# Where weight casts and inner operands stand in a Strassen-like MoE kernel's orders

## Chip, cores and metric

One Trainium2 chip, one NeuronCore of it. The metric is the device time of one execution in microseconds (us), from three runs of the kernel; beside them stands one profiled execution, with its own time and its trace. All times below are of the kernel before the change.

## What is computed

Soft routing over eight experts: every token goes through every expert, and the results are added with the softmax of the router's logits as weights. There are 8192 tokens of 512 features, and each expert is a 512x2048 matrix.

```python
probs = softmax(router_logits)                      # (16, 512, 8)
for e in range(8):
    expert_out = np.matmul(x, expert_weights[e])    # (16, 512, 512) @ (512, 2048)
    output += probs[:, :, e:e+1] * expert_out
```

Since the weight of an expert multiplies a whole row of x, this is one matrix product: a row of the left operand is (p_0 x, p_1 x, ..., p_7 x) with 4096 entries, and the right operand is the eight expert matrices on top of each other. The left operand is built on chip in float16, transposed; sums are accumulated in float32.

## The kernel before

**Products.** The big product is taken apart by a Strassen-Winograd scheme of seven products, numbered r = 1 to 7. Their right operands are blocks of the weights (11, 12, 21, 22: which half of the experts, which half of the columns) or sums of such blocks; their left operands are made from rows 256 at a time, for 16 pairs q of such row blocks. A product (r, q) is 256 rows by 1024 columns with a depth of 2048. It is done by the same scheme once more, in seven **steps** (1, 5, 6, 2, 7, 3, 4). A step is eight matmuls of 128x128 by 128x512 on TensorE. What a step leaves in PSUM is added up on VectorE or copied by ScalarE (`post`).

**Left operands.** A product's left operand `Left` has four tiles: t0 and t1 (x times a probability, one VectorE instruction each, tile `z` from `xT` and `pT`), s2 (tile `d`, a difference of the halves of t0, used by step 6), and the inner operand **i** = t1 minus s2 (tile `z` from `z,d`), used by steps 7 and 3.

**Stages and slots.** Stages are lists of one or two products; their steps alternate. In a stage of two products there are 14 slots: slot 2j is step j of the first product, slot 2j+1 is step j of the second. Stages 0 to 5 are pairs of product 1; stage 6 is product 2 of q = 13 and product 1 of q = 14; stage 7 is product 2 of q = 14 and product 1 of q = 15; stages 8 to 14 are pairs of product 2; stage 15 begins product 5. "Slot (7, 11)" below is slot 11 of stage 7. Hooks put by `at(stage, slot, make)` run ahead of a slot's matmuls.

**Third level.** In stages 0 to 5 and 8 to 12 (`thirds`) steps 1 and 5 of both products are taken together by the scheme once more, on 256 columns (`Third`, `Split`). This takes the place of slots 0 to 3. Its left sums are the tile **s** (four parts), its right sums the tiles **t** (eight parts for the first such stage of a right operand, `splits[2].queue` at slot (7, 2)). In `run_third` the parts m are written "x5", "q7" and so on: x for step 1, q for step 5. The last two slots of the stage before (`held`) are run in between: x1 x5 q1 q5, held slot 12, x2 q2 x6 q6, held slot 13, x7 q7 x3 q3 x4 q4. After x6 and q6 VectorE adds two halves in PSUM (`ps` from `ps,d`), and x7 and q7 write the half that was read there.

**VectorE's order** is written out by hand. All of its instructions stay in program order. Work that isn't the evacuation of a slot is a `Task` with an estimated cost in a deque, `queue`; `later` appends one. After each slot's matmuls `slack` takes tasks from the front for as long as VectorE's estimated clock is 0.3 us behind TensorE's (1.73 us a slot); then the slot's own evacuation is issued. A step that wants a task's result calls `need`, which takes everything in front of it too. `run(stage)` begins with `queue_i` for the stage's products, which appends their i tasks; the left operands of the next stage (t0, then s, s2, t1) are queued behind slot 0 or the part of it in a third-level stage.

**Background sums** are tasks of weights. A `wedge` makes three right operands from blocks 12 and 22 (sums with block 11) for one quarter-block of the weights: two casts from the float32 weights in HBM into the two halves a and b of one `w` tile, then three sums, t3 = b - a (into a tile `u`), t1 = (block 11) - a, t2 = b + a, each sent to a DRAM tile `wd` for later. Six wedges stand at stages 4 to 9; their sums are queued at slot 11 of the same stage (the last one at slot (10, 6)). `odd_t` at slot (12, 5) queues three sums of twice the size for a seventh place.

**Queues and buffers.** GpSimd issues the casts, the stores of results (`out_dram`), the partial results of product 1 (`kept`) and the `wd` stores, in program order; an entry that waits for its data or its buffer holds up what stands behind it. SyncE fetches and transposes; ScalarE's queue carries fetches of kept weights. The tiles `w`, `s`, `t` and `o` share one pool of 15 buffers: which buffer a new tile gets is settled by the order of the allocations (`new_w`, the `s` in `Third.make`, `new_t`), and its first writer waits until the earlier tile there has been read for the last time, by a matmul or by a store's landing.

The helper lines that the profile names are L112 (any VectorE tensor_tensor), L126 (any GpSimd DMA), L132 (any matmul), L180 (a fetch of kept weights), L627 and L638 (copies by ScalarE), L712 and L716 (the third level's copies).

Of the kernel before, what the change touches and what calls it, by code (L numbers as in the profile page):

```python
# [31 lines left out]
def kernel(  # L32
# [78 lines left out]
    def tt(o, a, b, op):  # L111
        dve(nc.vector.tensor_tensor(out=o, in0=a, in1=b, op=op))  # L112
# [29 lines left out]
    def new_z():  # L142
        return zpool.tile([P, K8, HQ], f16, name="z", tag="z")
# [248 lines left out]
    queue = deque()  # L392
    clock = {"pe": 0.0, "dve": 0.0}

    class Task:
# [5 lines left out]
        def run(self):  # L401
            self.done = True
            clock["dve"] += self.cost
            self.make()
# [10 lines left out]
    def later(cost, make, first=False):  # L415
        t = Task(cost, make)
        (queue.appendleft if first else queue.append)(t)
        return t

    def slack(slot=SLOT):  # L420
        if clock["pe"] > 30.0:
            clock["dve"] = max(clock["dve"], clock["pe"])
        clock["pe"] += slot
        while queue and clock["dve"] < clock["pe"] - LAG:
            queue.popleft().run()
# [66 lines left out]
    class Left:  # L492
# [48 lines left out]
                tt(self.s2, self.t[0][:, :, ds(HP, HP)], self.t[0][:, :, ds(0, HP)], SUB)  # L541
            self.task["s2"] = later(0.61, make)

        def queue_i(self):
            if self.into is not None:
                self.queue_make(1)

            def make():
                self.i = new_z()
                two = "p k (h t) -> p h k t"  # L550
                tt(self.i.rearrange(two, h=2), self.t[1].rearrange(two, h=2),
                   self.s2.unsqueeze(1).to_broadcast([P, 2, K8, HP]), SUB)
            self.task["i"] = later(1.14, make)

        def op(self, p):
            need(self.task[{1: 0, 5: 0, 6: "s2", 2: 1, 4: 1, 3: "i", 7: "i"}[p]])
# [194 lines left out]
    def at(stage, slot, make):  # L751
        hooks.setdefault((stage, slot), []).append(make)
# [47 lines left out]
    def product(r, q, **how):  # L800
        left, loads = left_of(r, q)
        lefts[r, q] = left
        p = None
        if r == 1:
            def sink(tn, o):
                pool(kept_rows(q)(tn), o)
            p = Product(right[1], left, sink)
        elif r == 2:
            if q >= 13:
                base = products[1, q].o.__getitem__  # L810
            else:
                base = bases[2, q] = Base(kept_rows(q))
            p = Product(right[2], left, to_out(q, 0, 0), base)
        elif r == 5:
            bases[6, q] = m1 = Base(kept_rows(q))
            m1.task = {}

            p = Product(right[5], left, to_out(q, 1, 0))
        elif r == 6:
            m1 = bases[6, q]  # L820

            def base(tn):
                need(m1.task[tn])
                return m1.t[tn]
            p = Product(right[6], left, to_out(q, 0, 1), base)
            if q in KEEP:
                left.kept = dram.tile([P, 2, K8, HQ], f16, name=f"kept_left_{q}")
        elif r == 7:
            if q < 14:
                base = bases[7, q] = Base(lambda tn: out_rows(q, 0, 1, tn))  # L830
            else:
                base = products[6, q].o.__getitem__
            p = Product(right[7], left, to_out(q, 1, 1), base)
        elif r == 4:
            p = Product(right[4], left, to_out(q, 1, 0, accum_op=ADD), products[7, q].o.__getitem__)
        else:
            p = Product(right[3], left, to_out(q, 0, 1, accum_op=ADD), **how)
        p.loads = loads
        products[r, q] = p
        return p  # L840
# [54 lines left out]
    def before(stage, n):  # L895
        for make in hooks.get((stage, n), ()):
            make()

    def after(stage, n):
        if n == 1:  # L900
            queue_lefts(stage + 1)
        if n == late.get(stage, 1):
            start_loads(stage + 2)
        if n == 5:
            store_loads(stage + 1)
        if n == 7:
            finish_loads(stage + 2)

    def run_third(stage):
        t = thirds[stage]  # L910
        before(stage, 0)
        t.parts("x1", "x5", "q1", "q5")
        after(stage, 1)
        before(stage, 1)
        held.pop(0)()
        after(stage, 2)
        t.parts("x2", "q2", "x6", "q6")
        before(stage, 2)
        held.pop(0)()
        after(stage, 3)  # L920
        before(stage, 3)
        t.parts("x7", "q7", "x3", "q3", "x4", "q4")
        for p in THIRD:
            for product in (t.a, t.b):
                product.post(p)
        after(stage, 4)

    def run(stage):
        some = stages[stage]
        for p in some:  # L930
            p.left.queue_i()
        slots = [(p, i) for i in range(len(some[0].steps)) for p in some]

        def one(n):
            p, i = slots[n]
            before(stage, n)
            p.step(p.steps[i])
            slack()
            p.post(p.steps[i])
            after(stage, n + 1)  # L940
        first = 0
        if stage in thirds:
            run_third(stage)
            first = 4
        end = len(slots) - (2 if stage + 1 in thirds else 0)
        for n in range(first, end):
            one(n)
        for n in range(end, len(slots)):
            held.append(lambda n=n: one(n))
# [23 lines left out]
    some = product(6, 15)  # L973
# [5 lines left out]
    some = product(4, order7[-1])  # L979
# [28 lines left out]
    def wedge(kn, e):  # L1008

        t = new_w()  # L1010
        a, b = t[:, ds(0, C), :], t[:, ds(C, C), :]
        rows = ds(e * C, C)

        casts = [lambda: cast_w(12, kn, e, a), lambda: cast_w(22, kn, e, b)]

        def send(what, u):
            to_kept(what, kn, e, u)

        def t3():
            u = new_u().rearrange("p (c two) t -> p c (two t)", two=2)  # L1020
            tt(u, b, a, SUB)
            send("t3", u)

        def t1():
            tt(a, b11[kn][:, rows, :], a, SUB)
            send("t1", a)

        def t2():
            tt(b, b, a, ADD)
            send("t2", b)  # L1030
        return casts, [t3, t1, t2]

    def wedge_at(stage, slot, kn, e, then):
        made = []

        def begin():
            casts, made_ = wedge(kn, e)
            casts[0]()
            made.extend(made_ + casts[1:])

        def go_on():
            for make in made[:3]:
                later(1.14, make)
        at(stage, slot, begin)
        at(stage, slot + 4, lambda: made[3]())
        at(*then, go_on)

    b21, t1, t2, t3 = {}, {}, {}, {}
# [19 lines left out]
    sums_at(5, 8, 2, b21, (7,))  # L1068
    sums_at(5, 12, 2, b21, (4,))
    for i, (kn, e) in enumerate((kn, e) for kn in ((0, 0), (1, 0), (1, 1)) for e in range(2)):  # L1070
        wedge_at(4 + i, 3, kn, e, {5:(10,6)}.get(i,(4+i,11)))

    def fetch_at_w(stage, slot, of, what, kn):
        at(stage, slot, lambda: of.__setitem__(kn, fetch_w(what, kn)))
# [4 lines left out]
    made = {}  # L1079
# [236 lines left out]
    for k in range(len(stages)):  # L1316
        run(k)
# [28 lines left out]
```

## Time and profile before

| what | value |
|---|---|
| three runs | 1364.66, 1365.53, 1365.61 us; median 1365.53 |
| the profiled execution | 1364.02 us, with a span of 1362.1 us from its first to its last instruction |
| granted TensorE clock | 1.00 over the whole span |
| HBM | 214.47 MB read, 167.97 MB written, 281 GB/s over the span |
| DMA queues, share of 16 engines | software (GpSimd) 56.7%, SyncE 32.3%, ScalarE 8.0% |

In the lines of a timeline the first two numbers are start and length in us; then come engine, line, operation and the tiles (written <- read); "x" is how many instructions were merged, and the bracket says how long the engine had been idle and what ended it. "PEld" is the load of a matmul's stationary operand. The end of a matmul is modelled, so neighbours overlap by a little, and the time from start to start is what a matmul costs. A `q` behind an engine's name is a DMA issued by it. The end of stage 7 and the beginning of stage 8 lie between about 205 and 240 us of the span.

### The profile page before, as it was taken

What the parts mean: (1) busy time and instruction counts of PE and PEld (TensorE: products, weight loads), DVE (VectorE), ACT (ScalarE), POOL (GpSimd) and SP (SyncE); (2) the same over time, 40 slices, a digit from 0 to 9 for tenths busy, and PEclk for the clock granted to TensorE, in tenths of its full rate; (3) what the DMA queues carried; (4) which work ended last, traced back from release to release, by engine and by line L of the source; (5) the groups of instructions that cost most, each with busy time, mean ns of one, the idle gap of its engine ahead of it and who ended that gap; (6) DMA issues with size and microseconds to landing.
All of it is one profiled execution on the core that took longest, in us unless ns stands there. A gap on an engine that the chain in (4) does not pass through costs nothing.

```text
span 1362.1 us, 18545 instructions
## 1 busy us (share of the span) xinstructions
PE 1355.7 (100%) x6801; PEld 662.8 (49%) x6801; DVE 1149.8 (84%) x1415; ACT 203.6 (15%) x386; POOL 409.4 (30%) x644
## 2 busy tenths in 40 slices
PE   9999999999999999999999999999999999999998
PEld 4555545565444444444444444444444444456554
DVE  7976789988999788787887888888889797998873
ACT  3332311111011111111111100000000000123221
POOL 3123233322223333324332122332333322232232
PEclk9999999999999999999999999999999999999999
DMA  9999999999999999999999977988898979999897
GB/s 192 229 249 247 232 232 310 286 309 356 314 307 273 315 339 286 294 280 281 328 275 334 351 241 206 221 246 204 230 243 234 241 204 296 291 223 247 198 206 117
DMA packets 195691, 356.43 MB, mean 262 GB/s; under 512 B 53136, under 2 KB 87184, under 8 KB 191248
## 3 DMA queue, kind: packets, MB, share of 16 engines
q0 software_dynamic: 88048, 183.02, 56.7%
q1 hardware_dynamic: 99488, 132.25, 32.3%
q10 hardware_dynamic: 8064, 39.99, 8.0%
q8 instruction: 53, 0.87, 0.3%
q14 instruction: 38, 0.31, 0.1%
HBM read 214.47 MB, written 167.97 MB: 281 GB/s over the span
## 4 chain that ended last, share of the span: by engine, by line
PE 98%; DMA 1%; issue 1%; POOL 0%; DVE 0%; ACT 0%; POOLq 0%
PE ps L132 98%; DMA w<-in_expert_weights_dram 1%; DMA out_dram<-h 0%; POOL w L126 0%; POOL kept L126 0%; POOL out_dram L126 0%; DVE h L112 0%; ACT h L638 0%; ACT h L1270 0%; DVE ps L112 0%; POOL ident L216 0%; POOLq L126 0%; POOLq L216 0%; POOLq L1330 0%
## 5 line engine op out<-in xcount | busy, mean ns | idle before, releaser
L132 PE MATMUL ps<-w,z 128*128 128x512 f16 x5144 | 1098.4, 373 | 0.4 <-DMA w<-in_expert_weights_dram 0.3
L132 PEld LDWEIGHTS <-z 128*128 128x128 f16 x5280 | 516.4, 98 | 578.1 <-DMA w<-in_expert_weights_dram 0.5
L126 POOL DMA_DIRECT2D out_dram<-h x380 | 249.4, 662 | 739.5 <-ACT h L638 366.1
L112 DVE TENSOR_TENSOR h<-ps,h 128x512 f32<-128x512 f32 x415 | 284.3, 687 | 157.5 <-PE ps L132 137.2
L112 DVE TENSOR_TENSOR z<-xT,pT 128x2048 f16<-128x2048 f16 x216 | 261.7, 1218 | 2.9 <-DMA xT<-w 2.9
L132 PE MATMUL ps<-w,d 128*128 128x512 f16 x880 | 199.1, 379 | 0.0
L132 PEld LDWEIGHTS <-d 128*128 128x128 f16 x880 | 86.1, 98 | 100.3
L112 DVE TENSOR_TENSOR z<-z,d 128x2048 f16<-128x2048 f16 x110 | 131.6, 1217 | 0.0
L638 ACT COPY h<-ps 128x512 f32<-128x512 f32 x64 | 37.6, 587 | 492.5 <-PE ps L132 486.8
L112 DVE TENSOR_TENSOR w<-w 128x1024 f16<-128x1024 f16 (+2 forms) x88 | 100.1, 1146 | 0.8
L627 ACT COPY h<-ps 128x512 f32<-128x512 f32 x90 | 52.8, 587 | 282.8 <-PE ps L132 267.2
L112 DVE TENSOR_TENSOR d<-z 128x1024 f16<-128x1024 f16 x110 | 74.4, 687 | 1.4
L624 ACT COPY h<-ps 128x512 f32<-128x512 f32 x90 | 51.7, 590 | 126.7 <-PE ps L132 119.8
L126 POOL DMA_DIRECT2D kept<-h x56 | 30.6, 547 | 106.7 <-ACT h L627 72.7
L132 PEld LDWEIGHTS <-s 128*128 128x128 f16 x544 | 53.2, 98 | 10.8 <-issue 1.3
L126 POOL DMA_DIRECT2D wd<-w x78 | 46.5, 621 | 38.4 <-DVE w L112 32.6
L132 PE MATMUL ps<-t,s 128*128 128x256 f16 x408 | 55.7, 273 | 0.8 <-DVE ps L112 0.8
L126 POOL DMA_DIRECT2D w<-in_expert_weights_dram x65 | 48.8, 771 | 11.9 <-issue 8.0
L112 DVE TENSOR_TENSOR ps<-ps,d 128x256 f32<-128x256 f32 x68 | 28.4, 430 | 24.9 <-PE ps L132 24.8
L112 DVE TENSOR_TENSOR ps<-ps,h 128x512 f32<-128x512 f32 (+1 forms) x66 | 45.1, 687 | 4.4 <-PE ps L132 4.1
L112 DVE TENSOR_TENSOR u<-xT,pT 128x2048 f16<-128x2048 f16 x38 | 46.3, 1217 | 0.0
L112 DVE TENSOR_TENSOR h<-h 128x512 f32<-128x512 f32 (+2 forms) x69 | 45.2, 675 | 0.1
(63 smaller groups left out, 365.2 us busy)
## 6 DMA issues: line engine op xcount, KB each, us to landing
out_dram<-h POOLq DMA_DIRECT2D x380, 256.0 KB, 6.9
pT<-p_dram SPq DMA_DIRECT2D x125, 256.0 KB, 6.8
h<-kept SPq DMA_DIRECT2D x116, 256.0 KB, 7.9
w<-wd ACTq DMA_DIRECT2D x25, 1024.0 KB, 11.0
xT<-x SPq DMA_DIRECT2D x76, 256.0 KB, 6.5
w<-in_expert_weights_dram POOLq DMA_DIRECT2D x35, 512.0 KB, 10.4
wd<-w POOLq DMA_DIRECT2D x64, 256.0 KB, 6.3
h<-out_dram SPq DMA_DIRECT2D x60, 256.0 KB, 5.6
```

Source lines behind the costliest of these rows:

```text
L112: dve(nc.vector.tensor_tensor(out=o, in0=a, in1=b, op=op))
L126: note(nc.gpsimd.dma_start(out=o, in_=i, **how))
L132: note(nc.tensor.matmul(ps, z, w, start=start, stop=stop, skip_group_check=True))
L624: act(nc.scalar.copy(o[tn], q if p == 5 else x))
L627: act(nc.scalar.copy(o[TN[p]], b if p == 2 else x))
L638: act(nc.scalar.copy(o[tn], b))
```

## The change

Two things. The casts of four of the six wedges move: in stages 6, 8 and 9 from slots 3 and 7 to slots 2 and 6, in stage 7 from slots 3 and 7 to slots 5 and 6. Stages 4 and 5 keep slots 3 and 7. And in stages 7 to 14 (`FIRST`) the tasks of the inner operands i aren't appended to the queue, but inserted directly behind the last task in it that belongs to the left operands of the stage's own products, or at its front if there is none. In other stages they are appended as before.

```diff
-        def queue_i(self):
+        def queue_i(self, place=None):
             if self.into is not None:
                 self.queue_make(1)
+            if place is None or self.into is not None:
+                place = len(queue)
 
             def make():
...
-            self.task["i"] = later(1.14, make)
+            self.task["i"] = t = Task(1.14, make)
+            queue.insert(place, t)
...
+    FIRST = lambda stage: 7 <= stage < 15
+
     def run(stage):
         some = stages[stage]
-        for p in some:
-            p.left.queue_i()
+        mine = [t for p in some for t in p.left.task.values()]
+        place = max((i + 1 for i, t in enumerate(queue) if t in mine), default=0) if FIRST(stage) else None
+        for i, p in enumerate(some):
+            p.left.queue_i(None if place is None else place + i)
...
-    def wedge_at(stage, slot, kn, e, then):
+    def wedge_at(stage, slot, kn, e, then, apart=4):
         made = []
...
         at(stage, slot, begin)
-        at(stage, slot + 4, lambda: made[3]())
+        at(stage, slot + apart, lambda: made[3]())
         at(*then, go_on)
...
     for i, (kn, e) in enumerate((kn, e) for kn in ((0, 0), (1, 0), (1, 1)) for e in range(2)):
-        wedge_at(4 + i, 3, kn, e, {5:(10,6)}.get(i,(4+i,11)))
+        wedge_at(4 + i, (3, 3, 2, 5, 2, 2)[i], kn, e, (10, 6) if i == 5 else (4 + i, 11), 1 if i == 3 else 4)
```

## The prediction

> **What bounds the kernel now.** I read the engines' shares first, then who TensorE waited for, then busy time by windows, and last the timeline around the one place that these point at.
>
> ```profile
> PE 1355.7 (100%) x6801; PEld 662.8 (49%) x6801; DVE 1149.8 (84%) x1415; ACT 203.6 (15%) x386; POOL 409.4 (30%) x644
> ```
>
> ```profile
> PE every L94 <- DVE zero L91: 1.3, 1, 1.3
> PE ps L132 <- DVE ps L112: 0.8, 1, 0.8
> PE ps L132 <- DMA w<-in_expert_weights_dram: 0.3, 1, 0.3
> PE ps L132 <- DVE h L112: 0.3, 1, 0.3
> ```
>
> ```profile
> 200.00:250.00 50.00, 49.13 (x256) 24.74 (x254) 44.90 (x61) 6.56 (x13) 16.65 (x28) 1.00 1.03 282
> 350.00:400.00 50.00, 50.00 (x233) 22.68 (x232) 49.97 (x50) 3.25 (x6) 13.34 (x23) 1.00 1.04 317
> 500.00:550.00 50.00, 50.00 (x233) 22.69 (x232) 40.41 (x52) 7.01 (x12) 18.80 (x33) 1.00 0.99 297
> ```
>
> TensorE is the bound, at the full granted clock (the 1.00 of the windows). The list of waits is its whole list: three of the four are at the start, which the change doesn't touch, and one is a wait of 0.8 us for VectorE. In the windows (columns: length, then PE, PEld, DVE, ACT, POOL busy, clock, DMA share, GB/s) the stretch from 200 to 250 us lacks 50.00 - 49.13 = 0.87 us; the others are full. A full window holds 233 or 234 long matmuls, so one costs 50/234 = 0.214 us, and a step of eight 1.71 us. **So no order of VectorE's or GpSimd's work can win more than 0.87 us of the profiled execution**, 0.06%. What can be lost has no such limit: VectorE stands at 49.97 of 50.00 from 350 to 400 us.
>
> The lost 0.87 us lies at the end of stage 7 and the beginning of stage 8:
>
> ```profile
> 206.75 0.71 POOL L126 DMA_DIRECT2D wd<-w  x1 [0.46 <-DVE w L112]
> 209.16 0.78 POOL L126 DMA_DIRECT2D w<-in_expert_weights_dram  x1 [0.42 <-PE ps L132]
> 215.31 0.69 DVE L112 TENSOR_TENSOR s<-z 128x1024 f16<-128x1024 f16 x1 [3.12 <-DMA wd<-w]
> 215.60 11.22 PE L132 MATMUL ps<-w,z 128*128 128x512 f16 x52
> 218.41 0.56 POOL L126 DMA_DIRECT2D out_dram<-h  x1 [8.46 <-ACT h L638]
> 218.96 0.75 POOL L126 DMA_DIRECT2D w<-in_expert_weights_dram  x1
> 227.97 2.76 PE L132 MATMUL ps<-w,z 128*128 128x512 f16 x16
> 228.89 1.23 DVE L112 TENSOR_TENSOR u<-w 128x2048 f16<-128x2048 f16 x1
> 230.03 0.68 DVE L112 TENSOR_TENSOR h<-ps,h 128x512 f32<-128x512 f32 x1
> 230.57 1.04 PE L132 MATMUL ps<-t,s 128*128 128x256 f16 x8
> 230.63 2.48 DVE L112 TENSOR_TENSOR w<-w 128x2048 f16<-128x2048 f16 x2
> 231.44 1.89 PE L132 MATMUL ps<-w,z 128*128 128x512 f16 x8
> 233.02 0.68 DVE L112 TENSOR_TENSOR h<-ps,h 128x512 f32<-128x512 f32 x1
> 233.62 0.75 DVE L112 TENSOR_TENSOR ps<-ps,d 128x256 f32<-128x256 f32 x2
> 234.10 1.03 PE L132 MATMUL ps<-t,s 128*128 128x256 f16 x8 [0.77 <-DVE ps L112]
> ```
>
> Held slot 13 starts at 231.44 and ends 1.71 later, at 233.15. Part x7 could follow, but starts at 234.10: it waits for VectorE's pair at 233.62, which evacuates x6 and q6. Those were done by 231.44, so VectorE was some 2 us behind. It fell behind at 215.31: the tile s waited 3.12 us until a wedge's sum had been stored (store issued at 206.75), because s had been given that sum's buffer. The wedge's cast at 209.16, allocated just ahead of s, had got a buffer that TensorE had freed by then. From 215.31 on VectorE has no idle time up to 234: each row above starts where the one before it in its queue ends.
>
> **The change part by part.**
>
> *Stage 7's casts.* With the first cast at slot 5, s is allocated first and should get the buffer that the cast had, free by 209.16. VectorE reaches s at 215.31 - 3.12 = 212.19, so its wait is gone and the backlog is up to 3.12 us smaller. The cast now takes the other buffer:
>
> ```profile
> wd<-w POOLq DMA_DIRECT2D x1, 512.0 KB, 8.4
> ```
>
> This is the store of 206.75 (its row in the view of DMA issues, with the us to landing at the end), which lands at 206.75 + 8.4 = 215.15. GpSimd stands there until then; behind it are only the second cast and the store of 218.41, whose data comes later, so the wait costs nothing. The second cast, now at slot 6, also stands ahead of that store instead of behind it, and is issued at 215.15 + 0.78 = 215.9 instead of 218.96. Both casts must have landed before t3, the row `u<-w`. From t3's start to x7 it was 234.10 - 228.89 = 5.21 us without a gap, so x7 starts at 233.15 if the casts land by L = 227.94, and L - 227.94 later otherwise. How long do casts take?
>
> ```profile
> w<-in_expert_weights_dram POOLq DMA_DIRECT2D x1, 512.0 KB, 6.0
> w<-in_expert_weights_dram POOLq DMA_DIRECT2D x1, 512.0 KB, 9.8
> w<-in_expert_weights_dram POOLq DMA_DIRECT2D x1, 512.0 KB, 12.0
> w<-in_expert_weights_dram POOLq DMA_DIRECT2D x1, 512.0 KB, 12.9
> w<-in_expert_weights_dram POOLq DMA_DIRECT2D x1, 512.0 KB, 16.0
> ```
>
> These are the casts issued at 189.7 (stage 6), 209.16 (this place), 279.2 and 282.6 (two under way together), and 314.0 (the slowest near here). So L lies between 215.9 + 6.0 = 221.9 and 215.9 + 16.0 = 231.9. In the nearest place the duration is 9.8, for two together 12.0 and 12.9; I take 11.4, halfway between 9.8 and 12.9, so L = 227.3 and x7 waits for nothing. The ends are: the whole 0.87 us gained, or 231.9 - 227.94 = 4.0 us of waiting, 3.1 us worse than now.
>
> *The other casts.* In stages 8 and 9 the first cast moves up by one slot to a buffer long free, and the second ahead of the store of slot 6. In stage 6 the same:
>
> ```profile
> 194.23 0.56 POOL L126 DMA_DIRECT2D out_dram<-h  x1 [3.74 <-ACT h L638]
> 194.79 0.75 POOL L126 DMA_DIRECT2D w<-in_expert_weights_dram  x1
> 201.76 1.23 DVE L112 TENSOR_TENSOR u<-w 128x2048 f16<-128x2048 f16 x1 [0.81 <-DMA w<-in_expert_weights_dram]
> ```
>
> The store held the second cast back by 3.74 us, and VectorE then waited 0.81 us for it. That wait goes; the sums and the store of 206.75 come up to 0.8 us earlier, which brings L down by as much. On TensorE it is worth nothing by itself: no wait of its own stands there.
>
> *The inner operands.* They change places with background sums only where such sums are queued when a stage begins: t1 and t2 in stage 8, three wedge sums in stages 9 and 11, two of odd_t in stage 13. In stage 8 the two i (2.36 us, like the row below) take the place of the 2.48 us pair at 230.63, so the sum above stands. Nothing is added: VectorE does the same work in another order. What it protects is seen in stage 11:
>
> ```profile
> 310.41 10.96 PE L132 MATMUL ps<-w,z 128*128 128x512 f16 x52
> 312.36 2.36 DVE L112 TENSOR_TENSOR z<-z,d 128x2048 f16<-128x2048 f16 x2
> ```
>
> Slot 6 starts at 310.41, so slot 8, which needs the first i, at 310.41 + 2 x 1.71 = 313.83. That i ends at 312.36 + 1.22 = 313.58, 0.25 us ahead; it becomes some 2.5 us more. In this execution that gains nothing, since no wait is there.
>
> The price is that a sum comes two tasks later: two slots, 3.4 us. Its buffers come free later by as much, and GpSimd's store of it may hold up stores behind it. The tightest of these that I found is in stage 12:
>
> ```profile
> 312.75 0.73 POOL L126 DMA_DIRECT2D wd<-w  x1 [1.02 <-DVE w L112]
> wd<-w POOLq DMA_DIRECT2D x1, 512.0 KB, 8.7
> 322.95 0.42 ACTq L180 DMA_DIRECT2D w<-wd  x1
> 333.80 6.42 PE L132 MATMUL ps<-w,z 128*128 128x512 f16 x29
> ```
>
> That store lands at 321.45 and would now land at 324.9, so a fetch into its buffer would hold ScalarE up by 2 us. ScalarE's next copy belongs to slot 6, which starts at 333.80: covered. Without cover it would cost at most the 3.4 us. The i tiles take the buffers of the i of the stage before, last read in slots 10 and 11, ahead of the place to which they move: no wait, so zero, with 1.2 us (one i behind a matmul) as the bound.
>
> **The sum.** Of the profiled execution 1364.02 - 0.87 = 1363.15 us remain; 1.9 us of its time lie outside the span of 1362.1 and stay. The median of the runs is 1365.53, 1.51 above the profiled one; by the same 0.87 it becomes 1364.66, which I round to **1364.7**. A difference of 0.2% is 2.7 us; less can't be told from no change here. So the forecast is: a gain too small to count.
>
> **The rivals.**
>
> *Late casts.* Two casts start together at 215.15, when SyncE's fetches of partial results (from 219) compete with them, and L passes 227.94. At 12.9 us L = 228.8 and nothing is gained; at 16.0 it is 3.1 us slower, 1368.6. It becomes slower by 0.2% from L = 227.94 + 0.95 + 2.7 = 231.6 on. For it: the DMA share is 1.03 in this window. Against: the casts no longer stand behind a waiting store.
>
> *Casts one after the other.* The second is moved only once the first is through, each in its 9.8 us: L = 215.15 + 19.6 = 234.8, 6.9 us of waiting, 6.0 more than now: 1371.5. Against it: the pair issued at 279.2 and 282.6 landed at 291.2 and 295.5, 4.3 us apart. [...]
>
> *The buffers don't change hands.* If s is given the stored sum's buffer in its new place too, it waits for 215.15 less 0.8; x7 comes at best 0.8 us earlier: 1364.8 to 1365.5.
>
> *The runs hide more.* The profiled execution is 1.51 us faster than the median. If in other executions the thin margins (the 0.25 us of stage 11, or the casts) turn into waits, the change removes these as well: down to 1363.15, and 2.7 us of gain only if a run loses more than that difference.
>
> *Late sums.* In the saturated stretch from 350 us on, or through stores behind a late sum, the 3.4 us come out on TensorE once: 1364.7 + 3.4 = 1368.1. Against it: in stage 13 the two i (2.4 us) and one sum of 2.2 us only change places, and the load ahead of slot 6 is the same.
>
> **How the numbers follow.** The forecast has 0.56; late casts 0.20, of which 0.05 beyond 231.6; casts one after the other 0.02; buffers as before 0.08; runs that hide more 0.10, of which 0.04 beyond 2.7 us; late sums 0.04, half of it for the case that the 3.4 us come twice, which is beyond 2.7 us. Slower by over 0.2%: 0.05 + 0.02 + 0.02 = 0.09. Faster by over 0.2%: 0.04. Within: 0.87. The range goes from 1363.0, which takes in most of the runs that hide more, to 1366.8, where late casts with L up to 230 are in; left out are some 0.18.
>
> **What would show it.** Right: s starts without a wait for a store, some 3 us earlier; the two casts of stage 7 stand next to each other on GpSimd near 215; x7 follows held slot 13 without a gap; TensorE's list of waits has only the start. Wrong: `u<-w` of stage 7 waits for a cast beyond 228 (late casts); s still waits for a `wd` store; a new wait of TensorE for `z`, `t` or `ps` in stages 8 to 14, or more than 0.87 us missing in any window of 50 us.

## The result and the profile after

| | before | after |
|---|---|---|
| median of the runs | 1365.53 us (5 runs, 1364.37 to 1368.17) | 1370.0 us (5 runs, 1369.52 to 1372.02) |
| the profiled execution | 1364.02 us | 1372.02 us, with a span of 1370.0 us |

The ratio is 1.0037 with a 95% interval from 1.0025 to 1.0049: 4.5 us slower by the medians, where 0.9 us less were forecast. The profiled execution of after is the slowest of its five, so it shows 8.0 us.

The page of after, its engines' shares, and its list of what TensorE waited for (us in total, times, longest; the first two of its rows):

```profile
PE 1357.1 (99%) x6801; PEld 662.6 (48%) x6801; DVE 1149.5 (84%) x1415; ACT 203.5 (15%) x386; POOL 409.5 (30%) x644
```

```profile
PE ps L132 <- DVE h L112: 3.8, 2, 3.5
PE ps L132 <- DVE ps L112: 3.4, 3, 1.7
```

TensorE's busy time is 1.4 us longer (its clock, below), the others' are within 0.3 us of before. TensorE waits 7.2 us for evacuations by VectorE, where it was 1.1 us. Where, the windows of after show (length, then PE, PEld, DVE, ACT, POOL busy, clock, DMA share, GB/s):

```profile
200.00:250.00 50.00, 50.00 (x261) 25.37 (x260) 45.99 (x62) 6.55 (x13) 17.04 (x28) 1.00 1.05 289
350.00:420.00 70.00, 66.83 (x310) 30.22 (x309) 64.97 (x61) 7.00 (x12) 15.14 (x27) 1.00 0.97 287
400.00:450.00 50.00, 44.77 (x199) 19.79 (x198) 46.35 (x49) 6.66 (x13) 12.27 (x22) 0.97 0.92 278
```

The stretch from 200 to 250 us is full: the 0.87 us were won. From 400 to 450 TensorE lacks 50 - 44.77 = 5.23 us. Two stops of TensorE make it up, in its timeline:

```profile
420.33 8.75 PE L132 MATMUL ps<-w,z 128*128 128x512 f16 x32 [3.50 <-DVE h L112]
430.81 1.89 PE L132 MATMUL ps<-w,d 128*128 128x512 f16 x8 [1.73 <-DVE ps L112]
```

The first row has 32 matmuls in 8.75 us, where the same 32 behind a stop take 7.07 us in the runs e2 and e9 below. In the window behind the stop the granted clock is halved (the 0.50).

```profile
421.00:424.00 3.00, 3.00 (x8) 1.06 (x7) 3.00 (x5) 0.56 (x1) 0.65 (x2) 0.50 1.04 377
```

The records of the clock have it at half from 420.87 for 3.41 us. By my estimate that costs another 3.41 / 2 = 1.7 us, and 8.75 - 7.07 = 1.68 agrees. A third stop lies at the turn from stage 4 to 5:

```profile
162.42 1.03 PE L132 MATMUL ps<-t,s 128*128 128x256 f16 x8 [1.55 <-DVE ps L112]
```

Its code is the same in both kernels, and its length changes from execution to execution (0 to 1.55 us in the profiles below). So the 8.0 us of the two profiled executions are 5.23 + 1.71 + 1.55 - 0.87, and 0.4 at the start.

**Where the 5.23 us come from.** VectorE in the saturated stretch, from the windows of before:

```profile
350.00:420.00 70.00, 70.00 (x326) 31.78 (x325) 69.83 (x69) 7.60 (x13) 17.66 (x31) 1.00 0.99 302
```

Before, VectorE idles 70.00 - 69.83 = 0.17 us in 70 us; after, 70.00 - 64.97 = 5.03. VectorE's timeline of after has 4.86 of these as two waits, at its sums of right operand 6, for fetches of the kept t2:

```profile
395.36 2.29 DVE L112 TENSOR_TENSOR w<-w 128x4096 f16<-128x4096 f16 x1 [1.44 <-DMA w<-wd]
402.27 2.29 DVE L112 TENSOR_TENSOR w<-w 128x4096 f16<-128x4096 f16 x1 [3.42 <-DMA w<-wd]
```

The fetches went out late. ScalarE's queue of after, the fetch of slot (12, 4) and the three of stage 14; and that of before:

```profile
333.92 0.37 ACTq L180 DMA_DIRECT2D w<-wd  x1
...
382.89 2.10 ACTq L180 DMA_DIRECT2D w<-wd  x3
```

```profile
322.95 0.42 ACTq L180 DMA_DIRECT2D w<-wd  x1
...
376.53 2.72 ACTq L180 DMA_DIRECT2D w<-wd  x3
```

The link between 333.92 and 382.89 is SyncE. Its waits from 330 to 360 us, in after, begin with

```profile
SPq L123 <- DMA w<-wd: 8.5, 1, 8.5
```

L123 is the helper of all SyncE's fetches; the one that waited fetches partial results (`h` from `kept`) and has no use for a `w`. In the trace's records each DMA names the semaphore that it raises when it lands. The 518 DMAs of SyncE and the 40 of ScalarE in the trace of after name the same eight, and all 550 of them that have an earlier one on their semaphore were issued after that one had landed. The fifth of eight fetches of partial results, issued at 346.99, names the semaphore of ScalarE's fetch of 333.92 (118 for both). The eight, and the transposes of the next left operands behind them, in SyncE's timeline of after and then of before:

```profile
335.82 12.98 SPq L123 DMA_DIRECT2D h<-kept  x8
...
361.66 9.76 SPq L463 DMA_TRANSPOSE xT<-xs  x4
```

```profile
334.55 8.72 SPq L123 DMA_DIRECT2D h<-kept  x8
...
357.18 8.62 SPq L463 DMA_TRANSPOSE xT<-xs  x4
```

SyncE is 4.5 us late at 361.66, and the t2 fetches are 6.4 us late: the first of them waits in the same way, for the semaphore of a load that SyncE issued at 374.70 and that took 8.1 us. Upstream, the fetch of 333.92 waited for the last wedge's store. GpSimd's timeline of after, then of before:

```profile
312.73 0.54 POOL L126 DMA_DIRECT2D wd<-u  x1 [6.30 <-DVE u L112]
...
313.79 0.78 POOL L126 DMA_DIRECT2D w<-in_expert_weights_dram  x1
314.54 0.73 POOL L126 DMA_DIRECT2D wd<-w  x1
...
315.81 0.72 POOL L126 DMA_DIRECT2D wd<-w  x1
```

```profile
311.01 0.72 POOL L126 DMA_DIRECT2D wd<-w  x1 [4.93 <-DVE w L112]
312.75 0.73 POOL L126 DMA_DIRECT2D wd<-w  x1 [1.02 <-DVE w L112]
...
314.04 0.77 POOL L126 DMA_DIRECT2D w<-in_expert_weights_dram  x1
```

Since stage 11's i now go first, the wedge's sums come later, and both `wd<-w` stores fall behind the cast of slot (11, 7), where before they were ahead of it. The view of DMA issues of after has, for the store of 315.81 and the fetch of 333.92 (KB each, us to landing):

```profile
wd<-w POOLq DMA_DIRECT2D x1, 512.0 KB, 18.0
...
w<-wd ACTq DMA_DIRECT2D x1, 1024.0 KB, 13.0
```

The store lands at 315.81 + 18.0 = 333.8 instead of 321.45, the fetch at 333.92 + 13.0 = 346.9, and at 347.0 SyncE goes on. In the kernel before the fetch took 14.0 us and landed at 336.95, and SyncE's fetch on the same semaphore went out at 337.76: the order held there by less than 1 us.

### The profile page after: what moved, and what is told of

Read it like the earlier page. It is cut to its first block, busy times and chain, and to the rows that moved or that the text cites. A ratio compares the mean times of both kernels' runs of the same rounds, so it can differ in the third digit from the quotient of the medians.

```text
span 1370.0 us, 18546 instructions
## 1 busy us (share of the span) xinstructions
PE 1357.1 (99%) x6801; PEld 662.6 (48%) x6801; DVE 1149.5 (84%) x1415; ACT 203.5 (15%) x386; POOL 409.5 (30%) x644
## 4 chain that ended last, share of the span: by engine, by line
PE 83%; issue 8%; DMA 4%; POOL 2%; DVE 2%; POOLq 0%; ACT 0%; DVEq 0%
PE ps L132 83%; DMA out_dram<-h 2%; POOL out_dram L126 2%; DMA w<-wd 1%; DVE z L112 1%; DMA w<-in_expert_weights_dram 1%; DVE h L112 0%; DVE w L112 0%; POOL w L126 0%; POOL wd L126 0%; DVE u L112 0%; DVE d L112 0%; DVE ps L112 0%; POOLq L126 0%; ACT h L1277 0%
## 5 line engine op out<-in xcount | busy, mean ns | idle before, releaser
L132 PEld LDWEIGHTS <-s 128*128 128x128 f16 x544 | 53.2, 98 | 11.8 <-issue 2.3
```

What stands on the lines that cost most here:

```text
L132: note(nc.tensor.matmul(ps, z, w, start=start, stop=stop, skip_group_check=True))
```

## The experiments

Letters for theories are explained in each expectation. Each kernel ran in 5 to 12 executions against the kernel before on the same chip, and one execution of each was traced. The times are medians; the ratios and their intervals are estimated over the executions and aren't the quotients of the medians (in e2 these are 1370.49 and 1366.09 us). Edits are shown against the kernel named at their head.

**One half at a time.** The casts alone:

```diff
# kernel after
-    FIRST = lambda stage: 7 <= stage < 15
+    FIRST = lambda stage: False
```

> The changed kernel with the inner operands appended as before; only the four wedges' casts stand in their new slots. Theory A (queue): the loss of the whole change, 1370.0 against 1365.53 us, comes from stage 11, where the two i pushed the last wedge's sums and so their two stores behind the cast of slot (11, 7); the casts' move by itself only closes the gap at the end of stage 7. Then this run is at or a little below the kernel before: 1364 to 1365.5 us, s starts without a wait, and the fetch into the last wedge's buffer goes out near 323 us as before (333.92 in the changed kernel). Theory B (casts): the moved casts of stages 8 and 9 crowd the queue, delay the stores of results and with them SyncE's fetches (one went out at 278.73 instead of 273.48): then some 4 us of loss stay, 1369 to 1371 us.

The inner operands alone:

```diff
# kernel after
-        wedge_at(4 + i, (3, 3, 2, 5, 2, 2)[i], kn, e, (10, 6) if i == 5 else (4 + i, 11), 1 if i == 3 else 4)
+        wedge_at(4 + i, 3, kn, e, (10, 6) if i == 5 else (4 + i, 11))
```

> The changed kernel with all casts back in their old slots; only the inner operands are moved. Theory A (queue): nearly the whole loss is here, 1369 to 1371 us, with TensorE waiting 3 to 6 us around 420 us of the span and a fetch by ScalarE near 334 us. Theory B (casts): no loss, 1364 to 1366 us.

Casts alone: 1363.78 us, ratio 0.9989 [0.9971, 1.0007]. The i alone: 1370.49 us, 1.0017 [1.0000, 1.0035]. The windows from 400 to 450, casts alone first:

```profile
400.00:450.00 50.00, 49.28 (x230) 22.20 (x228) 45.30 (x50) 7.87 (x14) 12.32 (x23) 1.00 0.95 280
```

```profile
400.00:450.00 50.00, 43.73 (x203) 19.64 (x202) 46.18 (x49) 7.00 (x12) 12.67 (x23) 1.00 0.91 277
```

The loss belongs to the inner operands (6.27 us there, 0.72 with the casts alone). The casts do what was forecast of them: in e1 the stretch from 200 to 250 us is full (50.00 of 50.00), though the interval of its times doesn't exclude no change.

**Which stage.** Stage 11's i left out, stage 11's alone in the kernel before, and stage 13's left out:

```diff
# e3, kernel after; for e11 the 11 is a 13
-    FIRST = lambda stage: 7 <= stage < 15
+    FIRST = lambda stage: 7 <= stage < 15 and stage != 11
# e10, kernel after, and the casts as in the kernel before
-    FIRST = lambda stage: 7 <= stage < 15
+    FIRST = lambda stage: stage == 11
```

> The changed kernel with the i of stage 11 alone appended as before; stages 7 to 10 and 12 to 14 and all casts as in the changed kernel. Theory A (queue): the stores of the last wedge go out ahead of the cast of slot (11, 7) again, the fetch goes out near 323 us, and the time is 1364 to 1365.5 us. Theory C (saturation): the sums of odd_t that were put later in stage 13, where VectorE has no idle time, are what is late: then 1369 to 1371 us.

> The kernel before, with the inner operands of stage 11 alone placed first. Theory A (the two stores of stage 11's sums fall behind the cast of slot (11,7) on GpSimd's queue, so ScalarE's fetch of slot (12,4) is late and with it SyncE): both stores behind that cast, the fetch at 330 to 334 instead of 322.95, the three fetches of t2 at 379 or later, a loss of 1.5 to 4 us between 400 and 450, median 1366.5 to 1368.5. Rival C (it takes stage 13's late sums as well): the fetch of (12,4) late, but the fetches of t2 by 378 and no loss over 1 us; median 1365.5 to 1366.2.

> The kernel after, with the inner operands of stage 13 left at the end of the queue as in the kernel before. Theory A (stage 11 is what counts): the fetch of slot (12,4) at about 334 as in the kernel after, the three fetches of t2 at 381 or later, a loss of 3 to 5 us between 400 and 450, median 1368 to 1370. Rival C (stage 13 is needed): the odd store at about 352.7 as before, the fetches of t2 at 377 to 379, a loss under 1.5 us, median 1364 to 1366.

Without stage 11: 1365.63 us, 1.0001 [0.9987, 1.0015]; the fetch is back at 322.81, though the traced execution, one of the slower ones (1368.03 us), lost 2.75 us between 350 and 450. Stage 11 alone: 1368.07 us, 1.0021 [1.0005, 1.0037]. Without stage 13: 1369.43 us, 1.0019 [1.0004, 1.0035], and its profile has the late t2 fetches again (382.01) and 4.64 us lost between 350 and 450. So stage 11 carries the loss, and stage 13, whose sums had been called in question in the prediction, isn't needed for it. The profile of stage 11 alone is one of its quicker executions (1364.46 us) and lost nothing here, against the 1.5 to 4 us that theory A expected. Its fetch and its SyncE:

```profile
331.81 0.37 ACTq L180 DMA_DIRECT2D w<-wd  x1
```

```profile
w<-wd ACTq DMA_DIRECT2D x1, 1024.0 KB, 9.1
```

```profile
334.62 9.36 SPq L123 DMA_DIRECT2D h<-kept  x8
```

The fetch is nearly as late as in after, but took 9.1 us instead of 13.0, so SyncE's eight fetches lasted 9.36 us instead of 12.98 and the t2 fetches went out in time, at 375.72. The chain breaks or holds by a few us of a transfer's duration. That would explain why executions of this one kernel lie between 1363.9 and 1374.5 us; with one trace of each kernel it isn't shown.

**The order on GpSimd's queue.** The cast put behind both stores in the kernel after, and, the other way round, ahead of the last store in the kernel before:

```diff
# e4, kernel after, in the list of casts for the seventh place
-(11, 7, 22, 1)
+(11, 9, 22, 1)
# e5, kernel before
-(11, 7, 22, 1)
+(11, 6, 22, 1)
```

> The changed kernel with one more edit: the cast of slot (11, 7) moved to slot (11, 9), behind the last wedge's two stores on GpSimd; all i moved. Theory A (queue): the order of cast and stores on that queue is what counts, not the sums' 2 to 3 us: the last store lands some 9 to 10 us after its issue instead of 18, the fetch goes out by 328 us, and most of the loss is gone: 1364 to 1366.5 us. Theory D (the sums' own lateness, wherever the cast stands): 1369 to 1371 us.

> The kernel before with one edit: the cast of slot (11, 7) at slot (11, 6). Nothing else moves, no i and no wedge; on GpSimd the cast now stands ahead of the last wedge's last store, which was issued 1.3 us ahead of it. Theory A (queue): that order alone makes the loss: the store lands 16 to 18 us after its issue instead of 8.7, ScalarE's fetch into the buffer goes out near 330 us instead of 323, SyncE is held up behind it, and the time is 1367 to 1371 us with a wait of TensorE near 420 us. Theory E (the i themselves, or where VectorE's sums stand): no loss, 1364 to 1366.5 us.

e4: 1364.89 us, 0.9994 [0.9974, 1.0013], against after's 1370.0, and against 1370.49 of e2 on the same chip. GpSimd's timeline and ScalarE's queue of e4:

```profile
313.31 0.71 POOL L126 DMA_DIRECT2D wd<-w  x1 [0.19 <-issue]
...
314.81 0.71 POOL L126 DMA_DIRECT2D wd<-w  x1
...
316.86 0.78 POOL L126 DMA_DIRECT2D w<-in_expert_weights_dram  x1
```

```profile
326.76 0.37 ACTq L180 DMA_DIRECT2D w<-wd  x1
```

The stores now stand first, the fetch goes out 7.2 us earlier than in after, and 1.61 us instead of 5.23 are lost between 400 and 450. The i are in their new place: by the medians, moving one cast takes away nearly all of their cost. The t2 fetches still went out at 380.40, and three of its executions took 1370 to 1371 us, where six of the kernel before's 35 on that chip took 1370 to 1373.

e5 is a miss for the theory in its strict form: 1366.34 us, 1.0004 [0.9993, 1.0015], the fetch only at 328.35, the t2 fetches at 376.42 and nothing lost from 350 to 450. Its store behind the cast did land late. The last store's row in e4 (ahead of the cast) and in e5 (behind it):

```profile
wd<-w POOLq DMA_DIRECT2D x1, 512.0 KB, 11.8
```

```profile
wd<-w POOLq DMA_DIRECT2D x1, 512.0 KB, 14.0
```

So the order on the queue delays the store (8.7 us before), but in e5 by less than in after, and what follows didn't come about. The traces in which this fetch stands at slot (12, 4), e8 to e11 below among them, show where it does. Where it landed from 345.8 to 348.0 (e8, e9, after, e2, e11), TensorE lost 3.05 to 6.27 us between 350 and 450. Where it landed from 336.9 to 340.9 (e1, before, e3, e4, e5, e10), it lost 0 to 1.61 us, and in e3 2.75.

**The fetch of slot (12, 4).** Moved to slot (12, 9), in the kernel after (e6) and with the casts alone (e7), to take SyncE's wait for it away:

```diff
-        fetch_at_w(*(((11,8),(12,4),(13,0)))[i], t1, "t1", kn)
+        fetch_at_w(*(((11,8),(12,9),(13,0)))[i], t1, "t1", kn)
```

> The changed kernel with one edit: the fetch of slot (12, 4), which waited for the last wedge's buffer until 333.92 us, stands at slot (12, 9), some 5 us later than that; its data is wanted near 365 us. Theory A with the semaphore as its middle (SyncE stood from 338.5 to 347.0 because its next fetch uses the semaphore of ScalarE's fetch, which had gone out late): SyncE isn't held up by that fetch, and the time is 1364 to 1366.5 us, though the store lands as late as in the changed kernel. Theory F (the late store and its traffic do it, not the order of the fetches): 1369 to 1371 us.

> The casts in their new slots, no i moved, and the fetch of slot (12, 4) at slot (12, 9): the version that should beat both kernels if the fetch's place is a thin margin also without the moved i. Theory A: at or below the casts alone, 1362.5 to 1364 us, with fewer runs above 1368 us. If the fetch's place matters only when its buffer is late: as the casts alone, 1363.8 us.

e6: 1368.07 us, 1.0012 [0.9995, 1.0029], between the two expected ranges, with 2.79 us lost. SyncE's wait of 8.5 us is gone, but one for a load of x (8.3 us, 5.9 in the kernel before) took part of its place and the t2 fetches still went out at 381.30. e7: 1368.13 us, 1.0014 [1.0002, 1.0026], 3.41 us lost, though no i is moved: a later fetch costs by itself, against both forms of its expectation. The edit moves the delay more than it removes it, and separates nothing cleanly.

**The last link.** The first t2 fetch earlier (e8), and the sums that wait for the fetches later in VectorE's order (e9), in the kernel after:

```diff
# e8
-        fetch_at_w(last2, 2 + 2 * i, t2, "t2", kn)
+        fetch_at_w(*((13, 9) if i == 0 else (last2, 2 + 2 * i)), t2, "t2", kn)
# e9
-    sums_at(last2, 9, 6, t2, (5, 6))
+    sums_at(last2, 12, 6, t2, (5, 6))
```

> The kernel after, with the first of the three fetches of t2 (right operand 6) moved from slot (14,2) to slot (13,9). Theory A (in the kernel after these three fetches go out at 382.89 instead of 376.53, VectorE waits 1.44 and 3.42 us for them in front of its sums, and TensorE loses 5.23 us between 400 and 450): if the first goes out some 3 us or more earlier, VectorE's first wait for a fetch there goes, and the loss between 400 and 450 falls below 3 us; median 1366 to 1368. If the fetch stays where it is, because its buffer or its semaphore holds it, nothing changes and the run tells nothing. Rival B (VectorE is overloaded there by the changed order itself, the fetches only show it): loss 5 us again, median 1370.

> The kernel after, with the sums of right operand 6 queued at slot (14,12) instead of (14,9), so that VectorE comes to them later, the fetches as they are. Theory A: VectorE no longer waits for the first fetch (1.44 us) and less than 2 us for the second (3.42); the evacuations behind them come in time, and the loss of TensorE between 400 and 450 falls from 5.2 to under 2.5 us; median 1366 to 1367.5, unless the sums then come in front of stage 15's left operands, which would give a new wait of TensorE for z at its beginning. Rival B (VectorE is overloaded by the changed order itself): the same sums are done there, the loss stays at 4 to 6 us, median 1370.

e8: 1372.24 us, 1.0038 [1.0025, 1.0051], the median missed. The first fetch went out at 365.53, and VectorE no longer waits for t2, but for partial results. Its waits from 350 to 425 us:

```profile
DVE ps L112 <- DMA h<-kept: 2.6, 2, 1.7
```

So it isn't the t2 fetches as such: VectorE idled 3.13 us from 350 to 420, for other late transfers, and TensorE lost 3.05. The median is nearer to rival B's, and why it is even above after's stays open; e4, with the same order of the i, speaks against rival B. e9: 1366.32 us, 0.9998 [0.9984, 1.0013], the median as expected, 3.7 us better than after; its profile was one with more loss than expected (3.84 from 400 to 450), with 2.0 us of waiting for t2 and 2.7 for `h<-kept`. Slack at the end of the stretch helps most executions.

**Is it one for one?** From the windows of the profiles so far (idle: the window less DVE busy; lost: the window less PE busy):

| kernel | VectorE idle, 350 to 420 | TensorE lost, 350 to 450 | clock at half, us |
|---|---|---|---|
| before | 0.17 | 0 | 0 |
| casts alone (e1) | 0.17 | 0.72 | 0 |
| stage 11 alone (e10) | 0.17 | 0 | 0 |
| before, cast to (11, 6) (e5) | 0.17 | 0 | 0 |
| without stage 11 (e3) | 1.38 | 2.75 | 3.41 |
| cast to (11, 9) (e4) | 1.78 | 1.61 | 0 |
| fetch later (e6) | 3.08 | 2.79 | 3.41 |
| t2 earlier (e8) | 3.13 | 3.05 | 3.41 |
| casts, fetch later (e7) | 3.78 | 3.41 | 3.41 |
| after | 5.03 | 5.22 | 3.41 |
| inner operands alone (e2) | 6.30 | 6.27 | 0 |
| sums later (e9) | 6.50 | 4.92 | 0 |
| without stage 13 (e11) | 6.72 | 4.64 | 3.41 |

Of the seven rows from 1.78 down in which the sums have their old place, six agree within 0.4 us; e9 gave VectorE slack. Three rows don't fit, which I can't account for: e1 lost 0.72 us with no more idle time than before, in e3 1.4 us more come out than went in, and in e11 2 us less. (In e3 VectorE had idled 2.9 us more than before between 330 and 350 already, but in after 2.4 us.) The columns go together, but late transfers are in all rows with a larger idle time. So one experiment adds work to VectorE and touches no transfer; the two i of stage 13 are computed twice, which is added work:

```diff
# kernel before
-        def queue_i(self):
+        def queue_i(self, times=1):
...
-                tt(self.i.rearrange(two, h=2), self.t[1].rearrange(two, h=2),
-                   self.s2.unsqueeze(1).to_broadcast([P, 2, K8, HP]), SUB)
+                for _ in range(times):
+                    tt(self.i.rearrange(two, h=2), self.t[1].rearrange(two, h=2),
+                       self.s2.unsqueeze(1).to_broadcast([P, 2, K8, HP]), SUB)
...
-            p.left.queue_i()
+            p.left.queue_i(2 if stage == 13 else 1)
```

> The kernel before, with the two inner operands of stage 13 each computed twice into the same tile: two more VectorE instructions of 1.13 us, 2.27 us of work at about 357 to 360 us; no DMA, no order and no other instruction is changed. Theory D (VectorE is saturated from 350 to 420 us and its evacuations end there just in time, so what it loses comes out on TensorE one for one, less some 0.2 us of slack): TensorE loses 2.0 to 2.3 us between 400 and 450 at a wait for VectorE's ps or h, the first t2 fetch stays at 376 to 378, median 1367.4 to 1368.2. Rival E (late transfers cost the time, VectorE's waits are a side effect): no loss over 0.5 us, median 1365.3 to 1366.2.

1370.92 us, 1.0035 [1.0022, 1.0049]: as slow as after, and more than either side expected. VectorE's timeline, the windows and TensorE's timeline of that kernel:

```profile
356.68 2.48 DVE L112 TENSOR_TENSOR z<-z,d 128x2048 f16<-128x2048 f16 x2
...
359.68 2.47 DVE L112 TENSOR_TENSOR z<-z,d 128x2048 f16<-128x2048 f16 x2
```

```profile
400.00:450.00 50.00, 47.48 (x214) 21.06 (x212) 46.88 (x51) 7.69 (x14) 12.44 (x22) 0.97 0.92 263
...
426.00:429.00 3.00, 3.00 (x9) 1.07 (x8) 1.95 (x3) 0.00 (x0) 0.00 (x0) 0.51 0.87 226
```

```profile
425.68 3.48 PE L132 MATMUL ps<-w,d 128*128 128x512 f16 x8 [2.52 <-DVE ps L112]
```

The pairs take 2.48 + 2.47 us, where two single i took 2 x 1.22: 2.51 us more work, 2.52 us of loss, 66 us downstream. The t2 fetches were in time (375.94). VectorE idled 0.24 us from 350 to 420, so no late transfer can stand for the loss in this execution. By the windows the clock is at half for 3.41 us from 425.52, just ahead of the stop's end; the eight matmuls behind it take 3.48 us, where they take 1.89 behind a stop in e2, so 1.6 us more. That second price was in no expectation. The two make 4.1 of the 5.2 us between the medians; the traced execution is the second quickest of the five (1368.89 us), and what the slower ones lost besides isn't shown.

**A version that beats both.** The casts alone, with the later sums of e9:

> The casts alone, with the inner operands in their old order, and the sums of right operand 6 queued at slot (14,12) instead of (14,9). Theory D: in an execution where no transfer is late these sums are done in the same stretch and nothing is gained, profile within 1 us of the casts alone (1362.9); executions in which a fetch of t2 is late lose less, so fewer of them lie at 1368 and above; median 1363.0 to 1364.5. If the later sums come in front of stage 15's left operands, TensorE waits there for h or ps as in the same edit of the kernel after (0.81 us before 390, 1.44 at 418): median 1364.5 to 1366.

1362.8 us (11 runs, 1361.78 to 1366.49) beside 1365.74 us of the kernel before, ratio 0.9979 [0.9968, 0.9989], just below the expected range. Whether the later sums add anything to the casts alone isn't shown: the interval of e1 overlaps with this one. Its page and its windows:

```profile
PE 1354.2 (99%) x6801; PEld 662.2 (49%) x6801; DVE 1150.1 (85%) x1415; ACT 203.4 (15%) x386; POOL 409.3 (30%) x644
```

```profile
200.00:250.00 50.00, 50.00 (x263) 25.51 (x261) 46.54 (x62) 6.55 (x13) 17.43 (x29) 1.00 1.03 293
350.00:420.00 70.00, 70.00 (x326) 31.76 (x325) 69.15 (x68) 8.18 (x14) 17.29 (x30) 1.00 0.96 296
400.00:450.00 50.00, 50.00 (x233) 22.62 (x231) 46.16 (x51) 8.19 (x14) 12.47 (x23) 1.00 0.96 278
```

Both stretches are full, and VectorE could idle 0.85 us without loss. The 2.9 us between the medians are more than the 0.87 us that one profile could show, and only part of that is in the tail: executions of the kernel before on that chip reach 1368.3 and 1370.0 us, and none of this version goes beyond 1366.5. The quickest of each, 1363.48 and 1361.78 us, are 1.7 us apart too. Where the rest comes from isn't shown.

## Why the prediction was wrong

**Stage 7's casts: right.** Timeline of after:

```profile
207.19 0.72 POOL L126 DMA_DIRECT2D wd<-w  x1 [0.46 <-DVE w L112]
212.56 0.68 DVE L112 TENSOR_TENSOR s<-z 128x1024 f16<-128x1024 f16 x1
215.70 1.52 POOL L126 DMA_DIRECT2D w<-in_expert_weights_dram  x2 [6.51 <-DMA wd<-w]
226.33 1.22 DVE L112 TENSOR_TENSOR u<-w 128x2048 f16<-128x2048 f16 x1
```

The buffers changed hands: s has no wait, GpSimd stands 6.51 us for the store in its place, both casts go out together at 215.70 (forecast 215.15 and 215.9), and `u<-w` at 226.33 waits for nothing, ahead of the bound of 227.94. The gain is the 0.87 us worked out. Of the rivals, late casts, casts one after the other and unchanged buffers didn't happen.

**The step that failed** is the price of the moved sums: "a sum comes two tasks later: two slots, 3.4 us", with the store of 312.75 landing at 324.9. The place was right (that store, that fetch in stage 12) and the size was not. The store was issued 3.1 us later, at 315.81, but landed 12.4 us later, because it had changed places on GpSimd's queue with a cast and took 18.0 us instead of 8.7: the prediction let the store come later and kept its duration. The cover was wrong as well: the waiter named was ScalarE's next copy, while the one that suffered was SyncE, through the semaphore that its fetches share with ScalarE's. There the margin was under 1 us, where the prediction saw the time up to slot 6 at 333.80 as cover and put the term at nothing.

**Late sums, the rival that came true**, had a chance of 0.04 and a price of 3.4 us. It named the stretch and the mechanism, "through stores behind a late sum". The measured price by the medians is 1370.0 - 1364.66 = 5.3 us. The argument against it looked at stage 13 alone, which by e11 isn't needed for the loss, and the note that VectorE stands at 49.97 of 50.00 was made as a warning but given no price. e12 gives it: 2.52 us of loss for 2.51 of work, and 1.6 us more at half the clock.

**The runs hide more** didn't come out in the change. e13, which moves the casts and the sums, leaves room for it: 2.9 us by the medians where the profiled execution had 0.87 to give.

## What to carry to other kernels

Where an engine that evacuates for TensorE idles 0.17 us in 70, an edit upstream is priced by the idle time that it may bring there, in e12 one for one (2.52 us of loss for 2.51 of work). Slack behind the stretch helped in e9 (1366.32 us, after's median 1370.0), and so did a better order ahead of it in e4 (1364.89). A result can be late by more than its task was moved: the store here went out 3.1 us later and landed 12.4 us later. List a moved store with what it now stands behind on the queue, and take the landing from a store in that place (14.0 to 18.0 us behind the cast in e5 and after, 7.4 and 8.7 ahead of it before). Look then for every DMA that waits for that landing, on the other issuing engines too: SyncE's wait here was 8.5 us.

## What the runs showed of the hardware

**Seven stops of TensorE came with half the clock.** With stops of 2.5 to 3.5 us (2.52 in e12, 2.75 in e3, 2.79 in e6, 2.91 in e11, 3.05 in e8, 3.41 in e7, 3.50 in after) the granted clock was 0.50 for 3.41 us each time. In windows of 0.5 us of the profiles that stretch begins from 0.16 us before the stop's end (e12: 425.52 and 425.68) to 1.19 us after it (e7: 427.30 and 426.11). It doesn't follow from the stop's length alone: e2's stops of 2.85 and 3.41 us and e9's of 2.40 left the clock at 1.00. What decides it besides isn't shown. The longer stop of e2, in TensorE's timeline:

```profile
430.99 1.89 PE L132 MATMUL ps<-w,d 128*128 128x512 f16 x8 [3.41 <-DVE ps L112]
```

**Late fetches of ScalarE held SyncE up.** SyncE waited 8.5 us for one in after, 8.8 in e2 and e8, 9.6 in e9 and 10.7 in e11, for data that SyncE's fetch had nothing to do with. In after both DMAs name semaphore 118.

**Stores behind the cast on GpSimd's queue landed later.** The wedge's 512 KB stores landed 7.4 to 11.8 us after their issue where they stood ahead of the cast (before, e1, e3, e4, the first of e5), and 14.0 to 18.7 us after it where they stood behind (after, e2, e5's last, e8 to e11).
